# Rotary swap by ScalarE copies, an earlier compression branch, smaller GpSimd pieces and kept down weights in a two-layer hybrid attention kernel

## The chip, the cores and the metric

The kernel runs on one core of a Trainium2 chip. The metric is the device time of one execution in microseconds (us); the median over several executions is compared. Of the core's engines, TensorE (PE; its weight loads are listed apart as PEld) multiplies matrices into PSUM, VectorE (DVE), ScalarE (ACT) and GpSimd (POOL) work on vectors, and SyncE (SP) issues most of the DMA transfers. Every engine takes its own instructions in order.

## What is computed

Two layers of a transformer block over 512 tokens of width 1024, all in float32 (batch 1). Cut to what matters here:

```python
for l in range(2):
    h = rms_norm(x, g_pre_mix[l])
    q_nsa, kv_nsa, g_nsa, qkv_sb, g_merge = split(h @ w_in)
    q, k_cmp, k_slc, k_win = rope(...)        # x1*cos - x2*sin, x2*cos + x1*sin
    kc, vc = gelu(blocks(k_cmp) @ w1 + b1) @ w2, the same of v_cmp
    o_nsa = gated sum of three softmax attentions (compressed, selected, window)
    o_sb = stick_breaking_attention(...)
    m = (sigmoid(g_a)*(o_nsa @ w_proj_nsa) + sigmoid(g_b)*(o_sb @ w_proj_sb)) @ w_out
    x = x + rms_norm(m, g_post_mix[l])
    u = causal_conv(rms_norm(x, g_pre_ffn[l]) @ w_up)      # 2 x 2816 columns
    x = x + rms_norm((gelu(gate) * up) @ w_down, g_post_ffn[l])
```

With 512 tokens all eight selection blocks are kept, so the selected attention is a plain causal one.

## The kernel before, in words

Activations lie transposed: 128 features on the partitions, tokens along the row. A product of full precision is made of three matmuls, since both operands are split into a rounded part and a rest: `h_hi,whi`, `h_lo,whi` and `h_hi,wlo` (`gemm`, L382). A weight tile is 128x1024 numbers (512 KB). `Weights` brings it in by a DMA of SP's queue (`wraw`, L74), rounds it with ACT (`whi`, L105) and subtracts with DVE or, for 13 tiles of a layer that serve the attention stage, with POOL (`wlo`, L106). Three raw buffers and two split ones go round.

The stages of a layer are these.

- **Head.** Six weight tiles of `w_in` run over the first 256 tokens while the norm of the others is made, then over the second 256 (`head_first`, `head_second`). Their results stand in six PSUM banks (`bk`, tag with 6 buffers). Before the change the tiles are, in order, the keys of the selected and window branches, two query tiles, the compression keys and the compression values. `rope` turns a tile: ACT copies the bank into SBUF (`rf`, L616), four DMAs swap its groups of 32 partitions (`rs`, L619), and DVE multiplies with cosine and sine (L620, L623) and adds. Then come the token-major values of both branches (`acc4`, four banks of the same tag, 128x280 matmuls), and two more query tiles.
- **Compression.** `kd` gets the compression keys and values, four DMAs each spread them into `cstk` (L660), ACT and DVE split that into `cst` (L712, L713), and 32 matmuls of 132 columns (`cst` against `wh`) make the hidden layer.
- **Attention (NSA).** 32 steps (`Sub`), one for each pair of head and block of 128 queries, go through a pipeline: scores `S`, maximum (DVE `st`, L906), exponential (ACT `P`), scaling by the gate over the sum (DVE L921 and L922, POOL L924), transposes (`tp`), split (`pt`), product with the values (`pv`). Between them the scheduler puts matmuls of later projections, each of which fills the one PSUM bank named `f` and is taken out of it by DVE (`sbz` L781, `gate` L802). The softmax of the compressed branch (`cmp_scores`, tiles `cp` and `cm`, L854 to L870) is woven in, two of its parts in each of two steps.
- **Stick-breaking attention, projections, output.** Not touched by the change.
- **Feed-forward.** 44 up tiles with convolution and gate, then eight down tiles `m` of 22 k-blocks in chunks of 8, 8 and 6 (`DCH`). The last three, 5 to 7, run first over the first half of the tokens and then over the second (`TAIL_D`), so that the next norm (`chain`) can start; each of their chunks is loaded and split twice.

The order of instructions on each engine is set when the program is built: the scheduler of the tile framework lays them out by its own model of times, with parts marked as of high priority ahead. The program of each engine is fixed from then on, and every engine waits for semaphores where a datum or a buffer is not there.

Of the kernel before, what the change touches and what calls it, by code (L numbers as in the profile page):

```python
# [33 lines left out]
TAIL_D = 3  # L34

# [18 lines left out]
class Weights:  # L54
# [27 lines left out]
    def split(self, upto):  # L82
        while self.n_split <= min(len(self.items) - 1, upto):
# [4 lines left out]
            if fold:  # L88
# [8 lines left out]
                continue  # L97
            if dest is None:
# [5 lines left out]
            for c in ((slice(0, n),) if i else (slice(0, n // 2), slice(n // 2, n))):  # L104
                self.nc.scalar.copy(hi[:, c], raw[:, c])  # L105
                eng.tensor_sub(lo[:, c], raw[:, c], hi.bitcast(F)[:, c])  # L106
# [4 lines left out]
    def get(self):  # L111
# [3 lines left out]
        return self.parts.pop(i)  # L115

# [42 lines left out]
def run_kernel(ctx, tc, xT, pos, inv, vec, pew, cw1, w_m, w_vn, w_pr, w_o, w_u, w_d, xmid, rot, out):  # L159
# [25 lines left out]
    for l in range(DEPTH):  # L185
# [19 lines left out]
        for i in dts:  # L205
            k0 = 0
            for n in DCH:
                it(w_d[l, i, :, k0 * 128:(k0 + n) * 128], n * 128)
                k0 += n
# [314 lines left out]
    for l in range(DEPTH):  # L524
# [39 lines left out]
        banks = [bank() for _ in range(HEAD)]  # L564
        banks = banks[1:] + banks[:1]
# [15 lines left out]
        with temps(6) as ip:  # L581
# [28 lines left out]
            def rope(b, done):  # L610


                f = wk(nm("rf"))
                s_ = wk(nm("rs"))
                t = wk(nm("rt"))
                nc.scalar.copy(f, b)  # L616
                for p in range(4):
                    q = p ^ 1
                    nc.sync.dma_start(s_[p * 32:p * 32 + 32], f[q * 32:q * 32 + 32])  # L619
                nc.vector.tensor_mul(t, f, cosT)  # L620
# [46 lines left out]
            for i in head_second(banks, kept, n_pre=HEAD):  # L667
                b = banks[i]
                if i < 2:
                    k_tile(i, b)  # L670
                elif i < 4:
                    q_tile(i - 2, b)
                elif i == 4:
                    rope(b, kc_done)
                else:
# [9 lines left out]
            for n_kt in (3, 3, 2):  # L685
# [11 lines left out]
                flush_later()  # L697
                kt += n_kt
# [10 lines left out]

            for v in range(2):  # L710
                src = cstk[:, v].rearrange("p (m s) -> p s m", s=8)
                nc.scalar.copy(cst[:, v, 0, :, :66], src)  # L712
                nc.vector.tensor_sub(cst[:, v, 1, :, :66], src, cst.bitcast(F)[:, v, 0, :, :66])  # L713
# [21 lines left out]
            for v in range(2):  # L735
                part = ip.tile([64, 132], F, name=nm("cpart"), tag="cpart")
                sums = ip.tile([64, 66], F, name=nm("csum"), tag="csum")
                nc.scalar.copy(part, cps[v][64:128, :132])
                nc.vector.tensor_add(part, cps[v][:64, :132], part)
# [99 lines left out]
        with temps(0) as nt, pool("pn", space=PSUM) as pn:  # L839
# [43 lines left out]
            class Sub:  # L883
# [35 lines left out]
                def scale(self):  # L919
# [4 lines left out]
                    nc.gpsimd.tensor_mul(pv, pv, st[:, None, 2:4, None].to_broadcast([128, self.i + 1, 2, 128]))  # L924
# [50 lines left out]
            pcs, cps_ = {}, {}  # L975
            subs[0].scores()
            at_sub = lambda n: subs[n] if 0 <= n < N else None
            for n in range(N + 3):
# [21 lines left out]
                for g_ in range(2):  # L1000
                    d = n - 15 * g_
                    if d == 2:
                        cg = cmp_scores(g_)
                    if 2 <= d < 4:
                        next(cg)
                        next(cg, None)
                    if d == 4:
# [350 lines left out]
```

## Time and profile before

| | |
|---|---|
| median of 3 runs | 1656.5 us (1655.12 to 1657.21) |
| profiled execution | 1653.88 us, of which 1652.2 us are the span of the profile |
| mean granted TensorE clock | 0.989 |
| PE busy | 1609.0 us (97% of the span) |
| DVE / ACT / POOL busy | 1118.2 / 825.3 / 211.1 us |
| DMA | 159.42 MB moved, mean 96 GB/s |

A row of the timeline begins with the start and the duration in us; what stands in brackets is the time for which the engine was idle before it and what ended that. A row of the waits has the engine, what it waited for, the sum in us, how often, and the longest. A row of the windows has the length, then busy time and instructions of PE, PEld, DVE, ACT and POOL, then the granted clock of TensorE (1.00 is full speed), the share of DMA time and GB/s. A row of a group has the line, engine, operation, output and inputs with shapes and the count, then the busy time in us and the mean in ns.

### The profile page before, as it was taken

To read this page: it belongs to the slowest core of one execution; us is meant where nothing else is said; L and a number is where in the kernel's file an instruction comes from. 1 tells how busy PE (TensorE), PEld (TensorE's weight loads), DVE (VectorE), ACT (ScalarE), POOL (GpSimd) and SP (SyncE) were. 2 spreads that over 40 slices of the span, in tenths; PEclk is the share of its full clock that TensorE was granted. 3 is DMA by queue.
4 is the path that set the end of the run, shared out by engine and by line. 5 is a ranking of instruction groups with operands and counts; after the bars stand their busy time and mean duration, and the time that the engine had idled before them with its cause. 6 is when DMAs were issued, how large, how long until landed. Compare 5 with 4: busy or idle time off the path is not lost.

```text
span 1652.2 us, 23212 instructions
## 1 busy us (share of the span) xinstructions
PE 1609.0 (97%) x8970; PEld 1393.2 (84%) x8970; DVE 1118.2 (68%) x1659; ACT 825.3 (50%) x1338; POOL 211.1 (13%) x252
## 2 busy tenths in 40 slices
PE   9899999999999999999999999999999999999997
PEld 9878887888998888888998788878889988888896
DVE  8775676767578777733677666677676687776235
ACT  6555565654555444423555455575536454444233
POOL 0034442120000000000000453322200000000000
PEclk9989999999999999999999999999999999999999
DMA  6521112114412233333664211112153132322344
GB/s 228 152 77 52 39 39 64 52 64 141 132 61 88 91 102 91 97 93 107 195 204 129 71 44 47 39 64 64 52 180 114 39 99 93 102 91 95 98 128 141
DMA packets 53501, 159.42 MB, mean 96 GB/s; under 512 B 6544, under 2 KB 12176, under 8 KB 53392
## 3 DMA queue, kind: packets, MB, share of 16 engines
q1 hardware_dynamic: 51088, 152.00, 29.0%
q0 software_dynamic: 1296, 4.72, 0.8%
q8 instruction: 70, 1.15, 0.3%
q10 hardware_dynamic: 1008, 1.23, 0.3%
q14 instruction: 39, 0.32, 0.1%
HBM read 144.30 MB, written 4.72 MB: 90 GB/s over the span
## 4 chain that ended last, share of the span: by engine, by line
PE 82%; DVE 8%; ACT 5%; issue 2%; DMA 2%; POOL 1%; SPq 1%; ACTq 0%; DVEq 0%; POOLq 0%
PE bk L382 56%; PE f L382 15%; PE pv L382 3%; PE Z L382 3%; PE S L382 2%; PE tp L935 2%; POOL sbt L1034 1%; DVE wlo L106 1%; DVE st L906 1%; DMA rs<-rf 1%; DMA x<-in_xT 1%; ACT whi L105 0%; ACT sbt L226 0%; ACT sbt L1058 0%; ACT sbw L226 0%
## 5 line engine op out<-in xcount | busy, mean ns | idle before, releaser
L105 ACT CAST whi<-wraw 128x1024 fp32r<-128x1024 f32 (+2 forms) x235 | 241.2, 1027 | 342.7 <-PE bk L382 254.3
L106 DVE TENSOR_TENSOR wlo<-wraw,whi 128x1024 fp32r<-128x1024 f32 (+2 forms) x209 | 248.8, 1191 | 184.1 <-ACT whi L105 181.4
L382 PE MATMUL bk<-h_hi,whi 128*128 128x512 f32 (+1 forms) x768 | 286.5, 374 | 2.1 <-ACT f_t L1260 1.7
L382 PE MATMUL bk<-h_hi,wlo 128*128 128x512 f32 (+1 forms) x768 | 286.4, 374 | 0.0
L382 PE MATMUL bk<-h_lo,whi 128*128 128x512 f32 (+1 forms) x768 | 286.2, 373 | 0.0
L382 PE MATMUL f<-h_hi,whi 128*128 128x512 f32 x448 | 184.4, 412 | 11.7 <-DVE gate L802 9.2
L382 PE MATMUL f<-h_lo,whi 128*128 128x512 f32 x448 | 179.1, 400 | 0.0
L382 PE MATMUL f<-h_hi,wlo 128*128 128x512 f32 x448 | 178.6, 399 | 0.0
L382 PEld LDWEIGHTS bk<-h_hi,whi 128*128 128x128 f32 x768 | 145.6, 190 | 27.7 <-ACT f_t L1260 1.9
L382 PEld LDWEIGHTS bk<-h_hi,wlo 128*128 128x128 f32 x768 | 145.5, 190 | 25.4 <-DVE wlo L106 0.4
L382 PEld LDWEIGHTS bk<-h_lo,whi 128*128 128x128 f32 x768 | 145.6, 190 | 24.8
L382 PE MATMUL bk<-ah,wlo 128*128 128x256 f32 (+1 forms) x484 | 161.7, 334 | 2.4 <-DVE wlo L106 2.4
L382 PE MATMUL bk<-ah,whi 128*128 128x256 f32 (+1 forms) x484 | 160.4, 331 | 0.0
L382 PE MATMUL bk<-al,whi 128*128 128x256 f32 (+1 forms) x484 | 160.2, 331 | 0.0
L382 PEld LDWEIGHTS f<-h_hi,whi 128*128 128x128 f32 x448 | 86.4, 193 | 30.6 <-DVE gate L802 10.0
L382 PEld LDWEIGHTS bk<-ah,wlo 128*128 128x128 f32 x484 | 91.8, 190 | 12.5 <-DVE wlo L106 3.4
L1228 DVE TENSOR_TENSOR cu<-bk,r 128x512 f32<-128x512 f32 x88 | 60.2, 687 | 61.2 <-PE bk L382 60.9
L382 PEld LDWEIGHTS f<-h_hi,wlo 128*128 128x128 f32 x448 | 85.9, 192 | 18.5
L382 PEld LDWEIGHTS f<-h_lo,whi 128*128 128x128 f32 x448 | 86.5, 193 | 15.5
L382 PEld LDWEIGHTS bk<-ah,whi 128*128 128x128 f32 x484 | 91.9, 190 | 8.7
L382 PEld LDWEIGHTS bk<-al,whi 128*128 128x128 f32 x484 | 91.9, 190 | 8.7
L382 PE MATMUL bk<-h_hi,wh 128*128 128x256 f32 x512 | 96.0, 285 | 0.0
(241 smaller groups left out, 3174.3 us busy)
## 6 DMA issues: line engine op xcount, KB each, us to landing
wraw<-in_w_u SPq DMA_DIRECT2D x88, 512.0 KB, 3.5
wraw<-in_w_m SPq DMA_DIRECT2D x72, 512.0 KB, 3.3
wraw<-in_w_d SPq DMA_DIRECT2D x44, 512.0 KB, 3.5
wraw<-in_w_d SPq DMA_DIRECT2D x22, 384.0 KB, 3.1
wraw<-in_w_pr SPq DMA_DIRECT2D x16, 512.0 KB, 3.6
wraw<-in_w_o SPq DMA_DIRECT2D x16, 512.0 KB, 3.5
rs<-rf SPq DMA_DIRECT2D x56, 64.0 KB, 2.8
wraw<-in_cw SPq DMA_DIRECT2D x4, 512.0 KB, 4.6
```

The costliest lines, as they stand in the source:

```text
L105: self.nc.scalar.copy(hi[:, c], raw[:, c])
L106: eng.tensor_sub(lo[:, c], raw[:, c], hi.bitcast(F)[:, c])
L382: last_mm[0] = nc.tensor.matmul(o, a, b, start=first, stop=last, skip_group_check=True)
L906: nc.vector.tensor_reduce(self.st[:, 0:2], self.S[:, :self.n].rearrange("p (j b k) -> p b j k", j=self.i + 1, b=2), axis=AX.XY, op=OP.max, ...
L935: nc.tensor.transpose(tp[:, b * 128:(b + 1) * 128], self.P[:, (c + b) * 128:(c + b + 1) * 128], ident)
L1034: nc.gpsimd.affine_select(out=d, in_=d, compare_op=OP.is_gt, fill=0.0, base=0, pattern=[[1, 128]], channel_multiplier=-1)
L1228: nc.vector.tensor_mul(u, b, r2)
```

## The change

Six edits, in the order of the program:

1. `rope` no longer copies the bank as a whole and swaps by DMA: four ACT copies of 32 partitions bring the swapped groups from PSUM to their places, and DVE multiplies the cosine with the bank itself.
2. The head tiles change places: compression keys and values come first. The first of them stands in the bank `f`, so the head uses five banks of the tag `bk`.
3. The split of `cstk` is written into the loop over the value tiles, after its first weight tile. The two small steps after the compression product get two buffers and high priority.
4. POOL's instructions are cut: a weight rest into four pieces of 256 columns, the scaling of a step into one piece for each 128 keys of the two branches.
5. The compressed softmax takes one part in each of four steps, that of the second group starts two steps earlier, and `pv_pair` of a group waits in a list until the compressed weights are there.
6. For down tile 6 the first two chunks are split into the second-half columns of `h_hi` and `h_lo`, which nothing reads at that time, and are used again for the second half of the tokens: two loads and two splits fewer in a layer.

```diff
@@ Weights.split
+            if isinstance(dest, tuple):
+                hi, lo = dest
+                raw = raw.rearrange("p (s c) -> p s c", c=256)
+                self.nc.scalar.copy(hi.whole(), raw)
+                eng.tensor_sub(lo.whole(), raw, hi.whole().bitcast(F))
+                self.parts[i] = dest
...
-                eng.tensor_sub(lo[:, c], raw[:, c], hi.bitcast(F)[:, c])
+                step = (c.stop - c.start) // (4 if eng is self.nc.gpsimd else 1)
+                for c_ in range(c.start, c.stop, step):
+                    s = slice(c_, c_ + step)
+                    eng.tensor_sub(lo[:, s], raw[:, s], hi.bitcast(F)[:, s])
...
+class Strips:
+    def __init__(self, t, k):
+        self.t = t
+        self.k = k
+    def whole(self):
+        return self.t()[:, self.k:self.k + 4, 256:]
+    def __getitem__(self, key):
+        c, e = key[1].start, key[1].stop
+        return self.t()[:, self.k + c // 256, 256 + c % 256:256 + c % 256 + e - c]
...
-            for n in DCH:
-                it(w_d[l, i, :, k0 * 128:(k0 + n) * 128], n * 128)
+            for c, n in enumerate(DCH):
+                keep = i == KEPT and c < 2
+                if not (keep and j >= 8):
+                    it(w_d[l, i, :, k0 * 128:(k0 + n) * 128], n * 128,
+                       dest=(Strips(lambda: h_hi, 4 * c), Strips(lambda: h_lo, 4 * c)) if keep else None)
...
-        banks = [bank() for _ in range(HEAD)]
-        banks = banks[1:] + banks[:1]
+        banks = [fbank("f")] + [bank() for _ in range(HEAD - 1)]
@@ rope
-                f = wk(nm("rf"))
-                nc.scalar.copy(f, b)
                 for p in range(4):
                     q = p ^ 1
-                    nc.sync.dma_start(s_[p * 32:p * 32 + 32], f[q * 32:q * 32 + 32])
-                nc.vector.tensor_mul(t, f, cosT)
+                    nc.scalar.copy(s_[p * 32:p * 32 + 32], b[q * 32:q * 32 + 32])
+                nc.vector.tensor_mul(t, b, cosT)
@@ loop over the value tiles (and taken out behind it)
+                if kt == 0:
+                    for v in range(2):
+                        src = cstk[:, v].rearrange("p (m s) -> p s m", s=8)
+                        nc.scalar.copy(cst[:, v, 0, :, :66], src)
+                        nc.vector.tensor_sub(cst[:, v, 1, :, :66], src, cst.bitcast(F)[:, v, 0, :, :66])
@@ Sub.scale
-                    nc.gpsimd.tensor_mul(pv, pv, st[:, None, 2:4, None].to_broadcast([128, self.i + 1, 2, 128]))
+                    for j in range(self.i + 1):
+                        nc.gpsimd.tensor_mul(pv[:, j], pv[:, j], st[:, 2:4, None].to_broadcast([128, 2, 128]))
@@ steps of the attention stage
-                    d = n - 15 * g_
+                    d = n - 13 * g_
                     if d == 2:
                         cg = cmp_scores(g_)
-                    if 2 <= d < 4:
-                        next(cg)
+                    if 2 <= d < 6:
                         next(cg, None)
-                    if d == 4:
+                    if d == 6:
                         pcs[g_] = cmp_transpose(g_)
                 if s3 and s3.hm == 1:
-                    pv_pair(s3)
+                    pv_due.append(s3)
+                while pv_due and pv_due[0].g in pcs:
+                    pv_pair(pv_due.pop(0))
@@ down_tile
+                    keep = m == KEPT and c < 2
+                    wt = kept_d[c] if keep and tr is HALVES[1] else W.get()
+                    if keep:
+                        kept_d[c] = wt
@@ _cols
-    tiles = [kv(2), kv(4), q(0), q(1), kv(0), kv(1), q(2), q(3)]
+    tiles = [kv(0), kv(1), kv(2), kv(4), q(0), q(1), q(2), q(3)]
```

Counted over the program, PE has the same 9011 instructions, ACT 38 more, POOL 174 more, DVE 4 fewer, and SP 60 fewer (the 56 transfers of the swap and four weight loads). What moves is shown at three places of the first layer.

**ACT at the end of the head.** The rows begin behind the load of `pew`. `rf` and `rs` are copies of `rope`, `kst` and `qst` the split keys and queries, `vN` and `gates` the values and gate columns, `cst` the split compression input. Before:

```order
L616 COPY rf_507<-bk_116 128x512
L616 COPY rf_545<-bk_117 128x512
L616 COPY rf_591<-bk_118 128x512
L650 CAST kst_5_105<-rt_509 64x4x128
L650 CAST kst_6_106<-rt_509 64x4x128
L616 COPY rf_638<-bk_119 128x512
L650 CAST kst_5_105<-rt_547 64x4x128
L650 CAST kst_6_106<-rt_547 64x4x128
L704 ACTIVATE vN_732<-bk_733,rT_465 128x4x64
L704 ACTIVATE vN_732<-bk_734,rT_465 128x4x64
```

Now:

```order
L647 COPY rs_507<-f_115 32x512 x4
L737 ACTIVATE vN_722<-bk_723,rT_465 128x4x64
L647 COPY rs_577<-bk_117 32x512 x4
L737 ACTIVATE vN_722<-bk_724,rT_465 128x4x64
L741 ACTIVATE gates_111<-bk_723,rT_465 128x24
L647 COPY rs_620<-bk_118 32x512 x4
L729 CAST cst_473<-cstk_472 128x8x66
L741 ACTIVATE gates_111<-bk_724,rT_465 128x24
L647 COPY rs_665<-bk_119 32x512 x3
L678 CAST kst_5_105<-rt_578 64x4x128
L678 CAST kst_6_106<-rt_578 64x4x128
L647 COPY rs_665<-bk_119 32x512
```

One copy of 128 partitions has become four of 32; the compression keys (`f_115`) come first, and the two splits into `cst`, which stood 12 and 15 rows behind those shown of before, now stand among the copies of the other tiles.

**PE at the compression product.** `f_` is a tile of a later projection, `bk_887` the last query tile, the rows of 128x132 are the compression product. Its surroundings before:

```order
L382 MATMUL f_2182<-h_lo,whi_951 128x512
L382 MATMUL f_2182<-h_hi,wlo_952 128x512
L382 MATMUL bk_933<-cst_473,wh_63_722 128x132 x16
L382 MATMUL bk_934<-cst_473,wh_69_839 128x132 x16
L382 MATMUL f_2227<-h_hi,whi_2207 128x512
L382 MATMUL f_2227<-h_lo,whi_2207 128x512
```

Now:

```order
L413 MATMUL bk_887<-h_lo,whi_659 128x512
L413 MATMUL bk_887<-h_hi,wlo_660 128x512
L413 MATMUL bk_919<-cst_473,wh_56_704 128x132 x16
L413 MATMUL bk_920<-cst_473,wh_64_833 128x132 x16
L413 MATMUL f_2216<-h_hi,whi_937 128x512
L413 MATMUL f_2216<-h_lo,whi_937 128x512
```

Before, a whole `f` tile (24 matmuls) stood between the last query tile and the product; now the product follows the query tile at once, and the first `f` tile comes behind it.

**DVE and POOL in the first steps of the attention stage.** `cp` and `cm` belong to the compressed softmax, `st` to the steps, `sbz` and `gate` take the bank `f` out. DVE before:

```order
L859 TENSOR_REDUCE cm_1096<-cp_1093 128x16
L921 RECIPROCAL st_1127<-st_1127 128x2
L860 TENSOR_TENSOR cp_1093<-cp_1093,cm_1096 128x512
L922 TENSOR_TENSOR st_1127<-st_1127,gates_111 128x2
L863 TENSOR_REDUCE cm_1096<-cp_1093 128x16
L864 RECIPROCAL cm_1096<-cm_1096 128x16
L867 TENSOR_TENSOR cm_1096<-cm_1096,gates_111 128x16
L802 TENSOR_TENSOR gate_2342<-f_2343,r_90 128x512
L868 TENSOR_TENSOR cm_1096<-cm_1096,rowv 128x16
L906 TENSOR_REDUCE st_1166<-S_1137 128x2
```

DVE now:

```order
L888 TENSOR_REDUCE cm_1099<-cp_1079 128x16
L950 RECIPROCAL st_1108<-st_1108 128x2
L889 TENSOR_TENSOR cp_1079<-cp_1079,cm_1099 128x512
L951 TENSOR_TENSOR st_1108<-st_1108,gates_111 128x2
L892 TENSOR_REDUCE cm_1099<-cp_1079 128x16
L893 RECIPROCAL cm_1099<-cm_1099 128x16
L810 SCALAR_TENSOR_TENSOR sbz_2379<-f_2345,r_90 128x512
L896 TENSOR_TENSOR cm_1099<-cm_1099,gates_111 128x16
L935 TENSOR_REDUCE st_1129<-S_1118 128x2
L897 TENSOR_TENSOR cm_1099<-cm_1099,rowv 128x16
L935 TENSOR_REDUCE st_1152<-S_1140 128x2
L818 TENSOR_TENSOR sbst_2301<-sbz_2379,sbst_2301 64x512
```

POOL before, and now:

```order
L106 TENSOR_TENSOR wlo_2331<-wraw_2217,whi_2330 128x1024
L924 TENSOR_TENSOR P_1133<-P_1133,st_1127 128x512
L106 TENSOR_TENSOR wlo_2369<-wraw_2256,whi_2368 128x1024
L924 TENSOR_TENSOR P_1172<-P_1172,st_1166 128x512
L106 TENSOR_TENSOR wlo_2401<-wraw_2295,whi_2400 128x1024
```

```order
L119 TENSOR_TENSOR wlo_2329<-wraw_2245,whi_2328 128x256 x4
L954 TENSOR_TENSOR P_1114<-P_1114,st_1108 128x256 x2
L119 TENSOR_TENSOR wlo_2371<-wraw_2251,whi_2370 128x256 x4
L954 TENSOR_TENSOR P_1136<-P_1136,st_1129 128x256 x2
L954 TENSOR_TENSOR P_1159<-P_1159,st_1152 128x256 x2
```

Before, the taking out of the bank (`gate_2342<-f_2343`) stood right behind the first product of the softmax factors `cm` with the gates; now `sbz_2379<-f_2345` stands ahead of that product, and the next one, `gate_2385`, eight rows behind what is shown. Each of POOL's rows of 1024 columns has become four of 256.

More of the change, by code (lines that the diff above doesn't have):

```diff
@@ L34 @@
 TAIL_D = 3
+KEPT = 6
 ALL = slice(0, T)
@@ L97, in split @@
                 continue
+            if isinstance(dest, tuple):
[4 more added lines that the diff above has]
+                self.parts[i] = dest
+                self.n_split += 1
+                self.prefetch()
+                continue
             if dest is None:
@@ L204, in run_kernel @@
         dts = list(range(8 - TAIL_D)) + 2 * list(range(8 - TAIL_D, 8))
-        for i in dts:
+        for j, i in enumerate(dts):
             k0 = 0
-            for n in DCH:
-                it(w_d[l, i, :, k0 * 128:(k0 + n) * 128], n * 128)
+            for c, n in enumerate(DCH):
[3 more added lines that the diff above has]
+                       dest=(Strips(lambda: h_hi, 4 * c), Strips(lambda: h_lo, 4 * c)) if keep else None)
                 k0 += n
@@ L668, in run_kernel @@
                 b = banks[i]
[L669 to L673, printed above, removed]
+                if i == 0:
                     rope(b, kc_done)
+                elif i >= 4:
+                    q_tile(i - 4, b)
+                elif i >= 2:
+                    k_tile(i - 2, b)
                 else:
@@ L708, in run_kernel @@
                 nc.scalar.activation(gates[:, j], acc4[j][:, 256:280], AF.Copy, scale=rj)
[L710 to L713, printed above, removed]
             qst.append(slot("q1", "qst1", FR))
@@ L735, in run_kernel @@
             for v in range(2):
-                part = ip.tile([64, 132], F, name=nm("cpart"), tag="cpart")
+                part = ip.tile([64, 132], F, name=nm("cpart"), tag="cpart", bufs=2)
                 sums = ip.tile([64, 66], F, name=nm("csum"), tag="csum")
-                nc.scalar.copy(part, cps[v][64:128, :132])
-                nc.vector.tensor_add(part, cps[v][:64, :132], part)
+                with tc.high_priority():
+                    nc.scalar.copy(part, cps[v][64:128, :132])
+                    nc.vector.tensor_add(part, cps[v][:64, :132], part)
                 nc.vector.tensor_add(sums, part[:, :66], part[:, 66:])
@@ L975, in run_kernel @@
             pcs, cps_ = {}, {}
+            pv_due = []
             subs[0].scores()
@@ L1253, in down_tile @@
                 k0 = 0
-                for n_ in DCH:
-                    drain(gemm(b[:, :w_], W.get(), *a_of(tr), range(k0, k0 + n_), first=k0 == 0,
+                for c, n_ in enumerate(DCH):
+                    keep = m == KEPT and c < 2
+                    wt = kept_d[c] if keep and tr is HALVES[1] else W.get()
+                    if keep:
+                        kept_d[c] = wt
+                    drain(gemm(b[:, :w_], wt, *a_of(tr), range(k0, k0 + n_), first=k0 == 0,
                                last=k0 + n_ == NF, ahead=2), side)
@@ L1260, in down_tile @@
                 nc.scalar.activation(f_t[:, m, tr], b[:, :w_], AF.Copy, scale=g_post2[:, m:m + 1])
+            kept_d = {}
             last = l == DEPTH - 1
```

## The prediction

> **What bounds the kernel now.** I read the page first, then PE's waits, then the windows for the granted clock, then the timeline at each wait.
>
> ```profile
> PE 1609.0 (97%) x8970; PEld 1393.2 (84%) x8970; DVE 1118.2 (68%) x1659; ACT 825.3 (50%) x1338; POOL 211.1 (13%) x252
> ...
> PE f L382 <- DVE gate L802: 9.2, 4, 4.0
> PE bk L382 <- DVE cst L713: 3.4, 2, 1.9
> PE bk L382 <- DVE wlo L106: 2.4, 3, 1.4
> PE bk L382 <- ACT wh L92: 2.4, 1, 2.4
> ...
> PE bk L382 <- ACT f_t L1260: 1.7, 1, 1.7
> ```
>
> PE is busy for 97%, and the change leaves its 9011 instructions as they are. So it can only win PE's 43 us of idle time and the time in which PE runs at a lower clock. The waits name the places: the bank `f` not taken out (9.2 us), the compression input (3.4), and some at the ends of the layers. The windows show the clock; the wait rows fall into them.
>
> ```profile
> 77.44:80.85 3.41, 1.53 (x12) 1.13 (x11) 3.12 (x5) 1.10 (x1) 0.00 (x0) 1.00 0.67 205
> 80.85:87.68 6.83, 6.83 (x30) 6.44 (x30) 5.57 (x9) 4.61 (x8) 0.34 (x1) 0.50 0.33 85
> 114.99:118.40 3.41, 1.19 (x7) 0.46 (x5) 2.71 (x5) 1.57 (x2) 2.28 (x2) 1.00 0.00 0
> 118.40:125.23 6.83, 5.04 (x12) 3.98 (x13) 3.89 (x8) 1.02 (x4) 2.14 (x2) 0.50 0.22 77
> 896.64:903.47 6.83, 6.83 (x27) 6.15 (x27) 6.51 (x11) 4.50 (x8) 0.59 (x1) 0.50 0.39 116
> 934.19:941.01 6.82, 5.67 (x13) 4.46 (x14) 3.25 (x8) 1.02 (x4) 1.50 (x2) 0.50 0.22 78
> 46.72:50.13 3.41, 1.66 (x13) 1.69 (x14) 3.33 (x5) 2.62 (x4) 0.00 (x0) 1.00 0.93 330
> ```
>
> Four stretches of 6.83 us run at 0.50, two in each layer, each behind a window in which PE had done little (1.53 of 3.41 us, 1.19 of 3.41). Busy time at 0.50 would take half as long at 1.00, so these stretches cost (6.83 + 6.83) / 2 = 6.8 us at the compression product and (5.04 + 5.67) / 2 = 5.4 us behind the `gate` wait, on top of the waits. The wait of the last window, at 48 us, was not followed by such a stretch.
>
> **The change, part by part.**
>
> *Compression input (edits 1, 2, 3).* The chain to the product in the first layer:
>
> ```profile
> 70.17 0.59 ACT L616 COPY rf<-bk 128x512 f32<-128x512 f32 x1 [1.54 <-DMA rs<-rf]
> 72.28 1.13 DVE L664 TENSOR_TENSOR kd<-rt,rs 128x512 f32<-128x512 f32 x1
> 73.44 2.42 SPq L660 DMA_DIRECT2D cstk<-kd  x4
> 77.36 1.18 ACT L712 CAST cst<-cstk 128x528 fp32r<-128x528 f32 x1 [2.70 <-DMA cstk<-kd]
> 79.82 6.13 PE L382 MATMUL bk<-cst,wh 128*128 128x132 f32 x32 [1.88 <-DVE cst L713]
> ```
>
> The compression keys were the fifth tile, so their copy came at 70.17. As the first tile, copied at about 48.4 (below), they reach `kd` before 54, and by the 5.1 us from the start of `kd` to that of `cst` plus two splits `cst` is there before 65. PE has values and two query tiles ahead of it, 96 matmuls of 280 columns and 48 of 512, about 24 us at 0.12 us for 256 columns (133 in 16 us, the window quoted next), and begins them at 46.1 (48.47 - 2.38, quoted next): it gets to the product at 70 or later. Both waits go: 3.4 us. With them the low windows go, and the product follows 48 dense matmuls: 6.8 us. If the wait stays, so do both.
>
> [...]
>
> *Rope (edit 1).* Durations of the copies from PSUM and of a split, behind the window of the rate:
>
> ```profile
> 830.00:846.00 16.00, 16.00 (x133) 15.89 (x133) 13.16 (x22) 9.89 (x17) 0.00 (x0) 1.00 0.70 214
> ...
> L616 ACT COPY rf<-bk 128x512 f32<-128x512 f32 x14 | 8.0, 588 | 16.6 <-DMA rs<-rf 9.5 <-DVE kst L651 7.1
> L1099 ACT COPY pvl<-pv 64x512 f32<-64x512 f32 x16 | 9.3, 584 | 8.0 <-PE pv L382 7.4
> L620 DVE TENSOR_TENSOR rt<-rf,cs_t 128x512 f32<-128x512 f32 x14 | 9.6, 691 | 3.6 <-DMA rs<-rf 2.1 <-ACT kst L650 1.4
> L1228 DVE TENSOR_TENSOR cu<-bk,r 128x512 f32<-128x512 f32 x88 | 60.2, 687 | 61.2 <-PE bk L382 60.9
> L650 ACT CAST kst<-rt 64x512 fp32r<-64x512 f32 x8 | 4.9, 618 | 2.0 <-DVE rt L643 1.6
> ```
>
> Half the partitions take the same time (584 against 588 ns), so a copy of 32 partitions, which no row shows, is put at 0.585 us; four are 2.34 us in place of 0.59, 14 times: 24.5 us more for ACT, which is busy for half the span. DVE's product reads a bank as fast as SBUF (687 against 691 ns), so nothing there. But until a bank is copied PE cannot write it again. In the first layer:
>
> ```profile
> 47.26 1.06 DVE L677 TENSOR_TENSOR kd<-bk,r 128x512 f32<-128x512 f32 x1
> 47.33 1.04 ACT L92 CAST wh<-wraw 128x1024 fp32r<-128x1024 f32 x1
> 48.47 0.36 PE L382 MATMUL bk<-wh,h_hi 128*128 128x280 f32 x1 [2.38 <-ACT wh L92]
> ```
>
> Before, the first value bank is the one that `kd` reads until 48.32, and PE stands for 2.38 us. Now it is the sixth buffer, free from the start, and the second is that of `kd`: 2.38 us won. A value bank takes 24 matmuls, 3.15 us, so PE wants the third at 46.1 + 6.3 = 52.4. That held the selected keys. ACT is free at 48.37 and by its order has four copies, one `vN` and four copies to do, 2.34 + 0.5 + 2.34, to 53.55, and DVE's product ends there too: a new wait of 1.2 us. The first query bank comes later: behind four more copies, a `cst` (1.18), three copies, two `kst` (1.24) and one copy, with small rows between, ACT is at 61, and DVE's product, which stands behind the `kst` rests, at 61.8. PE wants the bank 12.6 us of values and the first wait behind 46.1, at 59.9: 1.9 us. Sum 2.4 - 1.2 - 1.9 = -0.7 us. The ends: no new wait (+2.4), or all of five tiles' added ACT time on PE's path (2.4 - 5 x 1.75 = -6.4). I take -0.7, as it comes from the rows. In the second layer the tables are there earlier and a tile's copies (2.34 us) fit under its 24 matmuls of 256 columns (2.9 us): 0.
>
> *POOL's pieces and the softmax (edits 4, 5).*
>
> ```profile
> 108.12 2.39 POOL L106 TENSOR_TENSOR wlo<-wraw,whi 128x1024 fp32r<-128x1024 f32 x1 [2.34 <-ACT whi L105]
> 108.84 2.22 DVE L789 TENSOR_TENSOR sbst<-sbz,sbst 64x512 fp32r<-64x512 f32 x1 [0.69 <-ACT sbst L786]
> 117.16 2.34 POOL L106 TENSOR_TENSOR wlo<-wraw,whi 128x1024 fp32r<-128x1024 f32 x1 [0.40 <-ACT whi L105]
> 117.19 2.34 DVE L867 TENSOR_TENSOR cm<-cm,gates 128x16 f32<-128x16 f32 x1
> 119.45 0.68 DVE L802 TENSOR_TENSOR gate<-f,r 128x512 f32<-128x512 f32 x1
> 120.19 0.80 PE L382 MATMUL f<-h_hi,whi 128*128 128x512 f32 x1 [4.01 <-DVE gate L802]
> 197.41 2.06 POOL L924 TENSOR_TENSOR P<-P,st 128x256 f32<-128x256 f32 x2 [0.25 <-DVE cm L868]
> 197.45 1.12 DVE L870 TENSOR_TENSOR cp<-cp,cm 128x512 f32<-128x512 f32 x1
> ...
> L924 POOL TENSOR_TENSOR P<-P,st 128x1024 f32<-128x1024 f32 x16 | 30.3, 1896 | 31.5 <-PE pv L382 10.6 <-PE S L382 7.7 <-DVE st L922 7.1
> L924 POOL TENSOR_TENSOR P<-P,st 128x256 f32<-128x256 f32 x16 | 9.8, 615 | 26.2 <-PE tp L935 10.4 <-PE f L382 4.8 <-DVE st L922 4.3
> ```
>
> A DVE product of 16 columns takes 2.34 us, exactly as long as the POOL instruction beside it, and one of 64x512 takes 2.22 us until POOL is done. So a DVE instruction on two SBUF operands waits for the end of the POOL instruction that runs, and `gate`, for which PE stands 4.01 us, is queued behind it. At 197.41 DVE met two POOL instructions in a row; it was done at 198.57 and the pair at 199.47, so it got in between them. A piece of 256 columns takes 0.615 us, and so bounds such a wait; the two waits shown, up to 2.3 us each, shrink to at most 0.6 us each, which is about 3 of the 4.0 us of lateness. With the softmax spread, `sbz` also stands ahead of the `cm` product, and PE has two scores and a transpose to do before it wants the bank. I leave 0.3 us of each wait: 8.0 - 0.6 = 7.4 us, and with the low window the half clock goes: 5.4 us. If DVE does not get in between, both stay.
>
> The pieces cost POOL (1896 - 615) / 3 = 427 ns for 256 columns, so 188 ns for each further instruction; 174 more are 33 us. POOL has room (next fence). What hides it are the `f` matmuls between the steps; bare, all of the 96 further scaling pieces would lie on the way to the transposes: -18 us. On the other side, the attention stage's remaining idle time of PE could go: (168 - 160.35 - 4.01) x 2 = +7.3 us. I take 0, between, since the waits there come from DVE rows of both kinds.
>
> ```profile
> 90.00:258.00 168.00, 160.35 (x938) 134.76 (x937) 111.21 (x233) 90.13 (x231) 71.89 (x45) 0.98 0.15 49
> ```
>
> *Kept chunks and the bank of the first head tile (edits 6, 2).*
>
> ```profile
> 821.58 0.38 PE L382 MATMUL bk<-ah,wlo 128*128 128x256 f32 x1 [1.39 <-DVE wlo L106]
> ...
> 828.29 0.39 PE L382 MATMUL bk<-h_hi,whi 128*128 128x256 f32 x1 [1.67 <-ACT f_t L1260]
> ```
>
> The first is a wait for the last down tile's weights, one of three with 2.4 us in all. Two chunks whose split is already there give ACT and DVE two splits' time ahead of it; since the chain's DVE work stands between the splits as before, I take 1.7 of 2.4 (ends 0 and 2.4). The second is the head's first tile, which waits for a bank that the last `f_t` still reads. The bank `f` is free then, and only its weights can hold it: 1.5 us (ends 0 and 1.7).
>
> **Sum.** 3.4 + 6.8 - 0.7 + 7.4 + 5.4 + 1.7 + 1.5 = 25.5 us. The profiled execution (1653.88 us: a span of 1652.2 and 1.7 around it) would come to 1628.4. It lies 2.6 us under the median of the runs shown; the same gain from the median gives **1631 us**.
>
> **The rivals.**
>
> - *The half clock stays at the compression product.* For it: the product is of short matmuls, and the clock stayed at 0.50 through it. Against it: before each of the four stretches PE had idled. It returns 6.8 us: 1638.
> - *POOL's pieces run through.* POOL's four pieces stand in its queue with no wait between them; if DVE is let in only behind the last, the `gate` waits and their half clock stay: 1631 + 7.4 + 5.4 = 1644. Against it is the pair at 197.41, one case in a layer.
> - *More than forecast.* The attention stage's other waits (+7.3) and the new waits of the head (+3.1) go too: 1631 - 10.4, about 1620.
> - *Slower: POOL becomes the bound of the attention stage.* Each of its 132 pieces of a layer there (80 of scaling, 52 of weight rests) may itself have to wait for a DVE instruction. POOL's 71.9 us become 88 by the pieces. With a wait of 0.69 us each (a DVE product of 512 columns), they become 88 + 91 = 179, over the 168 of the stage: 22 us for two layers, and the gains of this part (12.8) are lost: 1631 + 12.8 + 22 = 1666. The point is where 2 x (88 + 132 w - 168) passes the 12.7 us left: w = 0.65 us. Against it: DVE is busy for two thirds of the stage, mostly with operands in PSUM.
> - *Nothing much.* The new order of the rows costs elsewhere what it wins.
>
> **How the numbers follow.** Chances: forecast 0.53, half clock 0.14, pieces run through 0.12, more 0.12, nothing much 0.03, slower 0.06. The range takes in 1620 and 1644 with their own spread of some 2 us: 1618 to 1646; what is left out is the slower case and tails of the others. What a measurement of this kernel can tell from no change is about 0.2%, 3.3 us. Faster: the first four, 0.91; same 0.03; slower 0.06.
>
> **What would show it.** Right: no stretch at 0.50 in the attention stage and the compression product (32 matmuls in about 3.5 us, not 6.1); the waits for `cst` gone; `gate` waits under 1 us; the products of `cm` under 0.8 us; a wait of 1 to 2 us for a third value bank and for the first query bank in the first layer alone; the head of the second layer without the wait for `f_t`. Wrong: a half clock behind a new wait in the head, DVE instructions as long as four POOL pieces, `tp` waiting for POOL's `P`, or an ACT copy of 32 partitions far from 0.585 us.

## The result, and the profile after

The changed kernel takes 1630.2 us (median of 4 runs, 1628.55 to 1632.35) against 1656.45 us (4 runs, 1655.12 to 1657.21): a ratio of 0.9843, 95% interval 0.9826 to 0.9860, or 26.2 us less. The forecast was 1631 us. The profiled execution took 1632.35 us (span 1630.7) and is the slowest of its four; against the profiled one of before (1653.88 us) that is 21.5 us. The trace is read against this smaller number.

The page of the changed kernel (busy time of the engines), and its PE waits (sum in us, times, longest):

```profile
PE 1594.9 (98%) x8970; PEld 1385.8 (85%) x8970; DVE 1097.7 (67%) x1655; ACT 846.3 (52%) x1376; POOL 237.8 (15%) x426
```

```profile
PE f L413 <- DVE sbz L810: 6.0, 2, 3.1
PE f L413 <- DVE vS L854: 3.7, 4, 1.6
PE bk L413 <- ACT gates L741: 2.0, 1, 2.0
PE pv L413 <- DVE wl L1122: 2.0, 2, 1.4
...
PE f L413 <- DVE gate L831: 0.9, 1, 0.9
...
PE bk L413 <- DVE wlo L119: 0.5, 1, 0.5
```

Of the 9.2 us for `gate` 0.9 are left, and the 3.4 us for `cst` and the 1.7 us for `f_t` are gone. At the head of the list stands a wait that the forecast did not have: about 3 us in each layer for `sbz`, the first tile in bank `f`. The timeline shows where it lies (PE rows, then the DVE and ACT rows on which it hangs):

```profile
54.85 0.40 PE L413 MATMUL bk<-wh,h_hi 128*128 128x280 f32 x1 [2.04 <-ACT gates L741]
...
72.09 3.69 PE L413 MATMUL bk<-cst,wh 128*128 128x132 f32 x32
75.62 0.44 PE L413 MATMUL f<-h_hi,whi 128*128 128x512 f32 x1
...
81.94 1.28 ACT L663 ACTIVATE qst<-rt 64x512 fp32r<-64x512 f32 x2 [2.13 <-DVE rt L658]
82.60 1.40 DVE L664 SCALAR_TENSOR_TENSOR qst<-rt,qst 64x512 fp32r<-64x512 f32 x2 [0.37 <-ACT qst L663]
...
84.37 0.68 DVE L810 SCALAR_TENSOR_TENSOR sbz<-f,r 128x512 f32<-128x512 f32 x1
...
85.10 0.67 PE L413 MATMUL f<-h_hi,whi 128*128 128x512 f32 x1 [3.09 <-DVE sbz L810]
```

The product of 32 matmuls runs at full clock (3.69 us, before 6.13) and without a wait, and so PE has filled the first `f` tile and computed the first scores by 82 us. DVE still has the last query tile to turn and split (`qst` until 84.0) and takes the bank out at 84.37.

To add up what the list of waits leaves out, PE's lost time was summed by place: for every matmul the time to the start of the next, less the median of that time for its number of columns (112 ns for 132 columns, 227 for 512, and so on). Time at half clock is in these sums, and so are gaps too short for the list of waits. In us, first and second layer:

| place | before | changed |
|---|---|---|
| up to the first value matmul (first layer) | 8.9 | 6.9 |
| values and last query tiles | 2.6 / 1.8 | 2.4 / 0.7 |
| compression product, first `f` tile | 3.3 / 3.3 | 0.0 / 0.0 |
| attention steps | 12.7 / 13.0 | 6.9 / 5.2 |
| stick-breaking heads behind them | 5.9 / 5.9 | 10.3 / 9.9 |
| output and up projections | 1.7 / 1.8 | 0.5 / 1.6 |
| down projection, head tiles behind it | 5.5 / 2.4 | 1.5 / 1.1 |
| sum | 68.8 | 46.9 |

The difference, 21.9 us, is within 0.4 us that of the profiled executions. Every place won but one: the stick-breaking heads, whose code the change does not touch, lost 4 us a layer more, 1.7 of it at half clock (half of a stretch of 3.41 us, an estimate). Ahead of the last matmuls the changed kernel has three stretches at 0.50, of 3.41 us each (at 85.27, 276.41 and 1095.61 us: behind the first `sbz` wait and once in the heads of each layer), where before there were four of 6.83 us.

### The profile page after: what moved, and what is told of

It reads as the page before. It is cut to its first block, busy times and chain, and to the rows that moved or that the text cites. A ratio compares the mean times of both kernels' runs of the same rounds, so it can differ in the third digit from the quotient of the medians.

```text
span 1630.7 us, 23349 instructions
## 1 busy us (share of the span) xinstructions
PE 1594.9 (98%) x8970; PEld 1385.8 (85%) x8970; DVE 1097.7 (67%) x1655; ACT 846.3 (52%) x1376; POOL 237.8 (15%) x426
## 5 line engine op out<-in xcount | busy, mean ns | idle before, releaser
L413 PE MATMUL bk<-h_hi,whi 128*128 128x512 f32 (+1 forms) x736 | 276.3, 376 | 0.6 <-ACT whi L115 0.6
L413 PE MATMUL f<-h_hi,whi 128*128 128x512 f32 (+1 forms) x480 | 190.9, 398 | 12.9 <-DVE sbz L810 6.0
L413 PE MATMUL f<-h_lo,whi 128*128 128x512 f32 (+1 forms) x480 | 187.1, 390 | 0.0
L413 PE MATMUL f<-h_hi,wlo 128*128 128x512 f32 (+1 forms) x480 | 186.7, 389 | 0.0
L413 PE MATMUL bk<-ah,wlo 128*128 128x512 f32 (+1 forms) x420 | 142.6, 340 | 0.5 <-DVE wlo L119 0.5
L413 PE MATMUL bk<-ah,whi 128*128 128x512 f32 (+1 forms) x420 | 142.3, 339 | 0.0
L413 PE MATMUL bk<-al,whi 128*128 128x512 f32 (+1 forms) x420 | 142.2, 338 | 0.0
L954 POOL TENSOR_TENSOR P<-P,st 128x256 f32<-128x256 f32 x160 | 94.4, 620 | 107.2 <-DVE st L951 55.6
L976 DVE TENSOR_TENSOR pt<-tp,pt 128x512 fp32r<-128x512 f32 (+1 forms) x96 | 56.6, 595 | 54.5 <-ACT pt L974 45.3
L413 PEld LDWEIGHTS bk<-ah,wlo 128*128 128x128 f32 x420 | 79.6, 190 | 9.4 <-DVE wlo L119 0.7
```

Of the source, the lines that this page charges most:

```text
L413: last_mm[0] = nc.tensor.matmul(o, a, b, start=first, stop=last, skip_group_check=True)
L954: nc.gpsimd.tensor_mul(pv[:, j], pv[:, j], st[:, 2:4, None].to_broadcast([128, 2, 128]))
L976: nc.vector.tensor_sub(lo[:, :w_, self.hm], src, hi.bitcast(F)[:, :w_, self.hm])
```

## The experiments

The experiments are numbered as they were put on record and stand here in the order of the argument. Each is compared with the kernel before on the same chip (1657.0 to 1657.2 us there); ratios have 95% intervals.

**1. POOL's instructions whole again.**

```diff
-                step = (c.stop - c.start) // (4 if eng is self.nc.gpsimd else 1)
+                step = (c.stop - c.start) // 1
-                    for j in range(self.i + 1):
-                        nc.gpsimd.tensor_mul(pv[:, j], pv[:, j], st[:, 2:4, None].to_broadcast([128, 2, 128]))
+                    nc.gpsimd.tensor_mul(pv, pv, st[:, None, 2:4, None].to_broadcast([128, self.i + 1, 2, 128]))
```

> The changed kernel with GpSimd's instructions whole again: one weight rest of 1024 columns, one scaling of 256 to 1024 columns, everything else as changed. Theory A (the prediction's: a VectorE instruction on two SBUF operands stands until the running GpSimd instruction ends, so the size of the piece sets the gate wait): products of cm of 16 columns take about 2.3 us again, TensorE waits about 4 us a layer for gate, with a half clock behind it (2.7 us), and the 3.1 us a layer of other idle time that the attention stage lost come back: 1630 + 13 to + 19 = 1643 to 1649. Theory B (the spread softmax steps removed the gate wait, not the pieces): VectorE instructions are long again but no gate wait above 1 us: 1630 to 1634. Theory C (188 ns for each further piece cost more than they win): below 1629.

Measured 1640.9 us, 0.9904 (0.9887 to 0.9922): 10 us slower than the change, between the theories. Of the tile `cm`, durations in ns (least, median, most), first in this kernel, then in the changed one:

```profile
L896 DVE TENSOR_TENSOR cm<-cm,gates x4: 169/1071/1973, 111.6 to 978.3; 128x16 f32<-128x16 f32 x4
```

```profile
L896 DVE TENSOR_TENSOR cm<-cm,gates x4: 167/168/168, 109.6 to 971.5; 128x16 f32<-128x16 f32 x4
```

VectorE is held up again, and the attention steps lose 14.0 and 14.3 us, more than before the change (12.7 and 13.0). But `gate` is waited for only 0.9 us in all: the wait did not come back, a crowd of small ones did.

**2. The softmax in its old steps, POOL's pieces kept.**

```diff
-                    d = n - 13 * g_
+                    d = n - 15 * g_
-                    if 2 <= d < 6:
+                    if 2 <= d < 4:
+                        next(cg)
                         next(cg, None)
-                    if d == 6:
+                    if d == 4:
```

(`pv_pair` is called at once again.)

> The changed kernel with the compression softmax in its old two steps of two parts each, GpSimd's pieces kept. Theory A (pieces set the wait): the products of cm take under 0.9 us, the gate wait is at most 1.2 us a layer, no half clock there: 1630 to 1633. Theory B (the spreading removed the wait): about 4 us a layer and a half clock come back: 1630 + 13 = 1643. In between (each took half): 1636.

Measured 1635.2 us, 0.9869 (0.9854 to 0.9883). The wait for `gate` is 1.2 us for both layers, as theory A says, and the time is 5 us over the change, which it did not say. So each part alone removes the gate wait, and only undoing both should bring it back.

**5. Both undone.** The edits of 1 and 2 together.

> The changed kernel with GpSimd's instructions whole and the compression softmax in its old two steps: all of the change but its parts on POOL and the softmax. With either of the two alone undone the gate wait stayed under 1 us a wait. Theory A (each of the two alone is enough, the prediction's mechanism): with neither, a 16-column product of cm is queued again behind a weight rest of 2.4 us, TensorE waits about 4 us a layer for gate with 2.7 us of half clock, on top of the 7 us a layer that whole instructions cost in the attention stage: 1641 + 13 = 1654. Theory B (the gate wait went because the rows ahead of it moved with the compression product, not by these two): no gate wait above 1 us: 1640 to 1645.

Measured 1642.7 us, 0.9918 (0.9902 to 0.9934). The long wait is back, in both layers, with the half clock behind it. It is now a wait for `sbz`, since that is what DVE has queued behind the product of `cm` (POOL's, DVE's and PE's rows of this kernel, then the window behind them, with the granted clock as the third number from the end):

```profile
109.06 2.34 POOL L119 TENSOR_TENSOR wlo<-wraw,whi 128x1024 fp32r<-128x1024 f32 x1 [0.40 <-ACT whi L115]
...
109.09 2.34 DVE L896 TENSOR_TENSOR cm<-cm,gates 128x16 f32<-128x16 f32 x1
111.36 0.68 DVE L810 SCALAR_TENSOR_TENSOR sbz<-f,r 128x512 f32<-128x512 f32 x1
...
112.09 0.80 PE L413 MATMUL f<-h_hi,whi 128*128 128x512 f32 x1 [4.07 <-DVE sbz L810]
```

```profile
110.71:117.54 6.83, 5.45 (x13) 4.29 (x14) 4.91 (x10) 2.26 (x6) 1.73 (x2) 0.50 0.21 77
```

The mechanism is theory A's. The letter of theory B came true as well, no wait for `gate` above 1 us (the longest is 0.6) and a time within 1640 to 1645; but what it meant, that the new order of the rows removed the wait, did not: the order changed the tile that is late, and the wait stayed. The price is not theory A's: 1654 was expected, since the small waits of experiment 1 were added to the long one, and the two do not add. The lost time of the attention steps, without the long waits for bank `f` and the half clocks, shows how the two parts work on each other (us, first and second layer):

| | two old steps | spread over four |
|---|---|---|
| POOL whole | 5.0 / 5.1 (experiment 5) | 9.1 / 9.5 (1) |
| POOL in pieces | 6.0 / 6.0 (2) | 1.9 / 2.1 (the change) |

Spreading alone costs 4 us a layer in small waits; with the pieces it wins 4. In PE's list, the waits for `pt`, which DVE splits behind each transpose, are 3.3 us in experiment 5, 6.0 in 1, 5.2 in 2 and 0.5 in the change; which rows make DVE late there was not followed up.

**6. POOL's pieces alone, on the kernel before.** The first diff of 1, the other way round.

> The kernel before with GpSimd's instructions in pieces of 256 columns, and nothing else of the change. Theory A: the products of cm fall from 2.3 us to under 0.9, the gate wait from 4.0 us a layer to about 1, its half clock (2.7 us) goes, and some 3 us a layer of the attention stage's other waits: 1656.5 - 2 x 8.7 = 1639, if what follows gives nothing back; with 4 us a layer given back at the heads behind it 1647. Theory B (the pieces do not touch the gate wait): at most the other 3 us a layer: 1650 to 1656.

Measured 1644.2 us, 0.9922 (0.9907 to 0.9937): 13.0 us less, between the two values of theory A. The attention steps lose 6.0 and 5.9 us in place of 12.7 and 13.0; the other waits there are unchanged to 0.02 us, and the heads behind still lose 5.9. The prediction's terms for this part were 7.4 + 5.4 = 12.8 us. The steps thus won 13.8 us, but the profiled executions differ by 9.8 only: about 4 us were lost at other places, 2.9 of them ahead of the second layer's compression product, where PE waits 1.8 us for the rest of a weight tile. The prediction's question, whether DVE gets in between the pieces, is answered by two rows of this kernel:

```profile
116.81 3.27 POOL L109 TENSOR_TENSOR wlo<-wraw,whi 128x256 fp32r<-128x256 f32 x4 [1.15 <-ACT whi L105]
117.32 0.77 DVE L873 TENSOR_TENSOR cp<-cp,cm 128x512 f32<-128x512 f32 x1
```

A product on two SBUF operands that starts while four pieces run until 120.08 is done at 118.09.

**3. The swap by DMA again, the new order of the tiles kept.**

```diff
+                f = wk(nm("rf"))
+                nc.scalar.copy(f, b)
-                    nc.scalar.copy(s_[p * 32:p * 32 + 32], b[q * 32:q * 32 + 32])
-                nc.vector.tensor_mul(t, b, cosT)
+                    nc.sync.dma_start(s_[p * 32:p * 32 + 32], f[q * 32:q * 32 + 32])
+                nc.vector.tensor_mul(t, f, cosT)
```

> The changed kernel with the rotary swap by one ScalarE copy of 128x512 and four DMAs again, the new order of the tiles kept. Theory A (ScalarE's queue is the cause of the new waits: 7 tiles with 1.76 us more each, and no gap on ScalarE from 46 to 80 us): the wait for a third value bank (2.2 us) goes, the wait for sbz at the first scores (3.2 us a layer) falls under 1 us with the half clock behind it: 1630 - 2.2 - 4.5 - 1.7 = 1622. Theory B (the wait for sbz stands because the compression product no longer holds TensorE up, whatever the swap): only the 2.2 us go, and the DMAs' 2 us of latency can bring a wait for cst back: 1628 to 1632.

Measured 1636.3 us, 0.9875 (0.9859 to 0.9892), slower than both theories. The wait for the third value bank went, as both said. The wait for `sbz` grew, to 3.77 and 5.91 us:

```profile
879.99 0.69 DVE L653 TENSOR_TENSOR rs<-rs,cs_t 128x512 f32<-128x512 f32 x1 [1.63 <-DMA rs<-rf]
...
889.95 0.69 DVE L653 TENSOR_TENSOR rs<-rs,cs_t 128x512 f32<-128x512 f32 x1 [1.28 <-DMA rs<-rf]
890.67 0.69 DVE L666 SCALAR_TENSOR_TENSOR qst<-rt,qst 64x512 fp32r<-64x512 f32 x1
891.38 0.69 DVE L812 SCALAR_TENSOR_TENSOR sbz<-f,r 128x512 f32<-128x512 f32 x1
...
892.13 0.79 PE L413 MATMUL f<-h_hi,whi 128*128 128x512 f32 x1 [5.91 <-DVE sbz L812]
```

DVE waits for the DMAs of the last tiles, and `sbz` is queued behind. My theory, that ScalarE's added copies cause the `sbz` wait, fell: without them it is longer.

**4. The first `f` tile ahead of the compression product.**

```diff
+        it(w_m[l, 8])
         for v in range(2):
             it(cw1[l, :, v * 1024:(v + 1) * 1024], dest=hold(("vs0", "vs1")[v]), fold=16)
-        for i in list(range(8, 12)) + list(range(16, 24)) + list(range(32, 36)):
+        for i in list(range(9, 12)) + list(range(16, 24)) + list(range(32, 36)):
...
+            first_f = fbank("f")
+            drain(gemm(first_f, W.get(), *h_of(ALL), range(KD), ahead=2))
             cps = [bank(), bank()]
```

(`sb_pair` then starts from `first_f`.)

> The changed kernel with one tile of the attention projections (its weights and its 24 matmuls into bank f) put ahead of the compression product, nothing else. Both theories of the new wait for sbz agree that VectorE then has the 3.5 us of the product more to take the bank out: the wait of 3.2 us a layer and the half clock behind the first go: 1630 - 6.4 - 1.7 = 1622. If the lateness only moves on (to the first maxima and exponentials, which stand behind the same ScalarE and VectorE rows), 1627 to 1630.

Measured 1628.2 us, 0.9827 (0.9813 to 0.9842). No wait for `sbz` above 0.9 us is left and no half clock behind it (the attention steps of the first layer, 87.6 to 239.5 us, ran at 1.00). In lost time, 6.4 us of waits became 3.9 us of smaller ones (1.15 and 1.05 us in the first layer, 0.95 and 0.71 in the second), two of them behind `qst`. The profiled execution is 3.5 us shorter, the median 2. The cause of the wait is confirmed; 8 us had been expected, and the second reading (the lateness moves on) is the one that holds.

**8. As 4, and the value tiles' work ahead of the second half of the gate tiles.**

```diff
-... + list(range(16, 24)) + list(range(32, 36)):
+... + list(range(16, 20)) + list(range(32, 36)) + list(range(20, 24)):
...
             gate(ga, 0, "vs0")
-            gate(ga, 1, "vs1")
             sb_values()
+            gate(ga, 1, "vs1")
```

> The kernel with the first attention projection ahead of the compression product (1628.2), and the four value tiles' work put before the second half of the gate tiles, so that 45 matmuls of gate tiles stand at the first two heads behind the attention stage, where the change left 24. Theory A (what the attention stage gained is given back at these heads because their cover was used up and the values come late: 8.4 and 8.8 us of idle time there, 4.9 to 5.4 in the runs that had 45): 1628.2 - 2 x 3.5 - 1.7 for half clocks = 1620. Theory B (the chain of a head itself bounds that stage, whatever stands beside it): 1626 to 1629.

Measured 1622.1 us, 0.9789 (0.9775 to 0.9804): 6.1 us less than 4, nearer to theory A. Windows of the first layer (length, then busy time of PE, PEld, DVE, ACT and POOL): the attention steps and the heads behind them of the changed kernel, then the heads of this one:

```profile
81.00:241.60 160.60, 156.38 (x931) 132.58 (x930) 106.72 (x240) 92.89 (x234) 85.75 (x132) 0.99 0.16 53
241.60:347.90 106.30, 101.96 (x529) 86.26 (x528) 78.39 (x81) 61.73 (x65) 26.35 (x60) 0.98 0.18 55
```

```profile
240.10:339.30 99.20, 97.52 (x516) 83.12 (x514) 73.50 (x77) 60.62 (x63) 25.96 (x60) 1.00 0.19 59
```

Over the heads PE is idle for 4.3 us in the changed kernel and for 1.7 us here. Lost time there is 5.0 us a layer, in place of 10.3 and 9.9 (8.4 and 8.8 in experiment 4). In the changed kernel 24 matmuls of an `f` tile stand between the first heads' scores and their next product, and PE waits first for the transposed values (`vS`: 1.5 and 1.6 of the 3.7 us in its list of waits); here 45 stand there, and the values are made before.

**9. The value tiles early, alone, on the changed kernel.**

> The changed kernel with the work on the four value tiles ahead of the second half of the gate tiles, and nothing else (the compression product stays ahead of the first projection). Theory A (the heads lost 4.4 and 4.0 us because their cover was used up): their idle time falls from 10.3 and 9.9 us to about 5 a layer, the waits for sbz (3.2 us a layer) stay: 1630.2 - 8.4 = 1622, and with the first projection ahead, as already run, 1622.1 would then hold 2 us of its own, so 1622 to 1624. Theory B (it wins only with the other move): 1628 to 1630.

Measured 1627.6 us, 0.9822 (0.9807 to 0.9837). The heads lose 5.1 us in both layers, as theory A says, but the time fell by 3 to 4 us, not by 8, and lies just under theory B's 1628 to 1630. The small waits of the attention steps rose from 1.9 and 2.1 us to 3.2 and 3.3, the output and up projections of the first layer lost 1.4 us more, and of the 3.4 us of half clock that the heads no longer have, 1.7 came back elsewhere: it now stands behind both `sbz` waits (in the first layer the granted clock is 1.00 over the heads, 0.98 in the change, and 0.99 over the attention steps).

**7. Without the kept chunks.** `KEPT = -1`.

> The changed kernel with the two down chunks loaded and split twice, as before. By the prediction's term the waits at the last down tile come back: 1630 + 1.7 = 1632 (0 to + 2.4). If the whole 3.9 us that the first layer's down projection and the head behind it gained were the chunks': 1634. If DMA and splits had room: 1630.

Measured 1632.45 us, 0.9847 (0.9831 to 0.9864); the time cannot tell it from the change. The trace can: the waits for the last down tile's weights are as before,

```profile
PE bk L413 <- DVE wlo L119: 2.5, 3, 1.4
```

and the lost time around the down projections is 3.8 and 2.4 us in place of 1.5 and 1.1: 3.6 us in all, of which the first layer has 2.2. The profiled executions differ by 1.5 us only, since the heads lost 4.7 us less in this one; why was not followed up.

**10. As 8, and the first key tile of the first layer swapped by DMA.** `rope` gets the old path for this one tile.

> The kernel of 1622.1 us (first projection ahead, values early), and in the first layer the first key tile alone is swapped by one ScalarE copy of 128x512 and four DMAs. Theory A (the 2.2 us for a third value bank are ScalarE's eight copies of 32x512 ahead of it, 2.35 us for four): the wait falls under 0.5 us, and with the share of its window up the half clock behind it (1.7 us, where it falls) goes: 1618 to 1620. Theory B (something else of ScalarE's queue ends last there, the table load or the split of the value weights): the wait stays above 1.5 us: 1622.

Measured 1619.6 us, 0.9774 (0.9759 to 0.9788), the fastest of all. The wait for the third value bank (2.0 us in experiment 8) is gone from PE's list, as theory A says, and this profile has no half clock before its last matmuls (mean granted clock 0.997, 0.994 in the change). A wait of 1.5 us for `sbz` has come back in the first layer. The intervals of the two ratios overlap, so that the step of 2.5 us from 1622.1 is not shown by the time; what is shown is the wait that went.

**11. The change once more.**

> The changed kernel once more. Idle times by place within 0.3 us of the first profile. If a half clock falls by where a wait lies against a grid of 3.41 us, not by the wait alone, the stretches at 0.50 stand at other waits than in the first profile (there behind the first sbz wait, and at 276 and 1095 us): 1628 to 1632, between 1 and 5 of them at 1.7 us each. If they belong to the waits: the same three places.

Measured 1631.7 us, 0.9849 (0.9833 to 0.9866). The waits are those of the first profile to 0.1 us, the half clock lies elsewhere (two stretches, at 886.07 and 1094.28 us): windows around the `sbz` wait in the first and in the second layer, of the first profile and then of this one (the clock is the third number from the end):

```profile
81.86:85.27 3.41, 0.32 (x3) 0.17 (x2) 2.91 (x9) 3.26 (x6) 0.00 (x0) 1.00 0.00 0
85.27:88.68 3.41, 3.41 (x9) 2.67 (x10) 2.14 (x6) 3.35 (x5) 0.00 (x0) 0.50 0.43 138
883.99:887.40 3.41, 2.13 (x13) 1.51 (x11) 2.91 (x9) 1.44 (x3) 0.00 (x0) 1.00 0.10 41
887.40:890.81 3.41, 1.74 (x8) 1.43 (x9) 3.34 (x9) 3.36 (x6) 0.00 (x0) 1.00 0.00 0
```

```profile
80.52:83.93 3.41, 1.52 (x10) 1.12 (x8) 2.94 (x8) 2.01 (x4) 0.00 (x0) 1.00 0.00 0
83.93:87.35 3.42, 2.32 (x10) 1.95 (x11) 3.05 (x9) 3.37 (x5) 0.00 (x0) 1.00 0.11 18
882.65:886.07 3.42, 0.65 (x6) 0.41 (x4) 2.92 (x8) 2.94 (x6) 0.00 (x0) 1.00 0.00 0
886.07:889.48 3.41, 3.25 (x8) 2.58 (x9) 2.16 (x6) 3.37 (x4) 0.00 (x0) 0.50 0.30 90
```

The same wait of about 3 us was followed by half clock in the first layer of one execution and in the second of the other. Where it fell into one window (0.32 and 0.65 us busy of 3.41), the next ran at 0.50; where the grid cut it in two (2.13 and 1.74; 1.52 and 2.32), none did.

## Why the prediction was right in sum, and where it was not

The forecast's terms, and what the two profiles show in their place (us, both layers, from the table of places and the waits in it):

| term | forecast | measured |
|---|---|---|
| waits for `cst` | 3.4 | 3.8 |
| half clock at the compression product | 6.8 | 6.6 |
| rope and head | -0.7 | -0.3 |
| gate waits and the half clock behind them | 12.8 | 13.8 (experiment 6, attention steps) |
| other waits of the attention steps | 0 (-18 to +7.3) | +7.9 |
| new wait for `sbz`, half clock behind the first | not in the sum | -8.1 |
| stick-breaking heads | not in the sum | -8.4 |
| kept chunks, first head tile | 3.2 | 5.3 |
| output and up projections | not in the sum | +1.4 |
| sum | 25.5 | 21.9 |

- *Compression input*: right. Both waits and both half clocks went, and with the product at 3.69 us the rival in which the half clock stays has fallen. Experiment 3 keeps this gain without edit 1; no run takes edit 2 or edit 3 back alone, so which of the two it needs is open.
- *POOL's pieces*: right in mechanism and size. The pieces alone gave 13.0 us, and the rival that they run through is refuted by the DVE product done amid four of them. One of its rows was read too closely: the 64x512 product at 108.84 ends at 111.06 us, 0.55 us behind POOL's 110.51, so that about 1.5 of its 2.22 us were the wait. That the softmax's new steps also suffice against the gate wait was not seen.
- *Rope*: near in sum, and wrong in its parts. A copy of 32 partitions takes 0.579 us (0.585 forecast). The third value bank was waited for 2.0 us (1.2 forecast), released by `gates` of the first value tile behind the eight copies. ACT began those copies at 48.90, not at 48.37, and DVE's product of a tile starts only when the fourth copy has ended (at 51.28, behind copies from 48.90 to 51.25), where the forecast let both end together. The wait for a query bank did not come. What failed is the step to "0" for the second layer, and the like in the first: it looked only at banks that a tile's copies hold, not at what is late next. When PE no longer stands at the product, DVE's chain of the last query tiles is what it meets, at the next turn of bank `f`. The order of PE's rows, with the product ahead of the first `f` tile, is shown in the part on the change, and the forecast put no cost on it.
- *"I take 0, between"* for the rest of the attention stage was mis-sized by 7.9 us, a little past its upper end. The gain needs pieces and spread steps together (the table in experiment 5); about as much was then lost at the heads, which the sum did not look at.
- *Kept chunks and first head tile*: under-sized. Experiment 7 gives the chunks 2.2 of the first layer's 3.9 us and the second layer's 1.3, 3.6 in all where 1.7 were forecast; the other 1.7 us of the first layer are the head tile's (1.5 forecast).
- *POOL as the bound*: no. In the first layer's attention steps it was busy 85.75 of 160.6 us (88 forecast; the first window of experiment 8), and a weight piece took 0.78 us in the mean, 0.74 where nothing held it up: far from the 0.65 us of waiting for each piece at which the forecast would have turned into a loss.

The terms for the compression product and for POOL's pieces, 23.0 of the 25.5 us, were sound in mechanism and size. The rest of the total is luck: +7.9, +2.1 and +1.4 that the forecast did not have stand against -8.1 and -8.4 that it did not have either, which leaves 21.9. That the medians nevertheless differ by 26.2, and the forecast of 1631 us was met within 1 us, comes from the two profiled executions: that of before lay 2.6 us under its median and that of the change 2.1 over. The forecast for a profiled execution was 1628.4 us; the one of the change took 1632.35.

## What to carry to other kernels

When a wait is removed, follow PE to its next use of the same kind of bank and ask which engine's queue it now meets early: here moving 24 matmuls ahead of the product turned 6.4 us of new waits into 3.9. A gain in a stage that a scheduler fills with later work uses up the cover of the next stage; look there before booking it. Pieces of 256 columns on POOL and the spreading of the DVE work were worth more together than apart (1.9 and 2.1 us lost, against 6.0 and 6.0 with the pieces alone and 9.1 and 9.5 with the spreading alone), so test a pair of edits in all four combinations.

## What the runs showed of the hardware

The length of a wait alone does not sort the cases in which half clock followed: 1.88 us were followed by it in the kernel before, and of the waits for `sbz` of the changed kernel 3.09 and 2.93 us were (first layer of the first profile, second layer of experiment 11), while 2.95 and 2.99 us were not (the other layers). What differed there is how the wait lay against a grid. In the kernel before, the change and experiment 11 all stretches at 0.50 ahead of the last matmuls begin at multiples of 3.413 us from each other (80.85 and 118.40: 11 of them; 85.27 and 276.41: 56; 886.07 and 1094.28: 61) and last 3.41 or 6.83 us. In the two executions of the changed kernel the grid lies 1.3 us apart (a line of it at 85.27 in the first, at 83.93 in the second, counted back from 886.07). How little work in a window is followed by half clock is not shown: the stretches at 276.41 and 1095.61 came behind windows in which PE was busy for 2.39 and 2.02 of 3.41 us, and none came behind those with 1.74 and 1.52.

In the stretches at 0.50 a matmul of 512 columns followed the one before after 427 ns (median, before and changed), elsewhere after 227. A stretch of 3.41 us filled with them thus cost 1.6 us; the 1.7 us put on each in the experiments is half its length, an estimate.

A VectorE product on two SBUF operands stood until the GpSimd instruction beside it ended (2.34 beside 2.34 us in experiment 5, with 0.03 us between their ends), and another was let in between two of GpSimd's instructions though these waited for nothing (done at 118.09 amid four pieces that ran until 120.08, experiment 6).
